# Strassen's seven products for eight in the query, key and value projections of a two-layer attention encoder

## The chip, the core and the metric

The kernel runs on one core of a Trainium2 chip. The metric is the time of one execution on the device, in microseconds. The core has five engines with queues of their own: TensorE (PE in the profile, with PEld for its weight loads), VectorE (DVE), ScalarE (ACT), GpSimd (POOL) and SyncE (SP), which here issues nearly all DMAs. Each engine takes its instructions in the order in which they stand in the built program.

## The reference

512 tokens of 1024 columns pass two layers, everything in float32. Layer A is a dilated sliding-window attention with three head groups, layer B a neighbourhood attention on an 8 x 64 grid. Each layer normalises its input, projects it to queries, keys, values and a gate, attends, multiplies by the SiLU of the gate, projects back and adds the input.

```python
hn = rms_norm(x, norm_gain[i])
proj = hn @ w_in              # layer A: 3 groups x (q, k, v) x 1024 columns, and 1024 of gate
q, k = rms_norm(q, q_gain[g]), rms_norm(k, k_gain[g])      # per head of 64
o, lse = dilated_group_attention(q, k, v, t5_bias, dilation, reach)
y = softmax-weighted sum of the three groups' o, times silu(gate)
x = x + y @ w_out
```

## The kernel before

**Head pairs.** The 16 heads are worked two at a time, as eight pairs (`hc` 0 to 7) of 128 columns. For one pair of layer A the projection has 1280 columns: 1024 of queries, keys and the values of groups 1 and 2, in two blocks of 512, then 128 of the values of group 0 and 128 of the gate. `main_a(hc)` (from L493) issues `project_qk` twice, then `v0_a` and `gate_a`.

**Precision.** A float32 product is made of three products of a rounded high half and a low half (`mm3`, L212, matmul line L206): high by high, high by low, low by high. The activations' halves `hn_h` and `hn_l` lie in SBUF from the start. The weights are read from memory as `wraw` (128 x 1024, three buffers), and `split` (L124) makes 128 x 512 halves of them: ACT rounds into `wh` (L127), then DVE or POOL subtracts into `wl` (L131), two of five on POOL. Both have four buffers, and `splits` keeps four ahead of TensorE.

**The projection.** In `project`, for each of eight k blocks of 128 rows one half `wh`, `wl` is multiplied with four tiles of 128 tokens into four accumulators in PSUM. ACT evacuates them scaled by the tokens' norm `rs_n` (L444), POOL squares (L268), DVE reduces (L269). `head_norm` makes the per-head scale in some 14 small steps (`rsqrt`, on POOL for keys, on DVE for queries) and DVE applies it (L290).

**The attention of a pair.** `k_a` turns the scaled keys on TensorE (`transpose4`) into `k12`. `q_a` turns the queries on DVE (L519) and through memory: four writes to `qd` (L532) and four reads (L538), after which `split_q` makes `k0h`, `q0h` on ACT (L559, L578) and `k0l`, `q0l` on DVE (L561, L580). `attn_a` issues two blocks of scores (`u` 0 and 1), DVE adds the bias and takes the minimum (L748, L759), ACT takes the exponential (L770), DVE the reciprocal (L608), ACT scales (L609). DVE turns the probabilities in 32 x 32 blocks (L681), and a `turner` sends them through memory (`td`, L690; `pt`, L694). `weigh` multiplies them by the values into `o`, and `put_y` multiplies by the gate (L629) and splits the result into `y_h` and `y_l` in SBUF, which `out_product` reads.

**The order.** `main` yields the large matmuls and `side` the rest. `run` weaves the two by a clock of TensorE's own work (`clock`, in nanoseconds): `yield "wait", key, n` lets a side step go n ns of that work after a stamp, and `later_on` does so for DMAs. So TensorE's order is fixed by hand, without regard to what the other engines really take; on the other engines the order comes from a scheduler that goes by estimates. In before, the weighing of a pair is held in `pending` and comes in the middle of the next pair's attention, the keys are turned 18,500 ns after their projection, and the values `v0` have two buffers.

```python
yield "wait", ("rawk", hc), 12500 if hc == 0 else 25500 if hc == 1 else 18500 if hc < NHC - 1 else 10000
...
pending.append(lambda: put_y(hc, weigh(), True, False))
```

Of the kernel before, what the change touches and what calls it, by code (L numbers as in the profile page):

```python
# [31 lines left out]
EXT = S + 64  # L32

# [9 lines left out]
def tile_hybrid_encoder(  # L43
# [45 lines left out]
    ones = cp.tile([P, S], F32R, name="ones")  # L89
    nc.vector.memset(ones.bitcast(F32), 1.0)  # L90

# [6 lines left out]
    v0 = [cp.tile([P, 4, P], F32, name=f"v0_{i}") for i in range(2)]  # L98
# [3 lines left out]
    x_all = big.tile([P, KT, S], F32, tag="y", name="x_all")  # L102
    y_l = big.tile([P, KT, S], F32R, name="y_l")
# [18 lines left out]
    turn, pool = [0], [2, 5]  # L122

    def split(raw, n):  # L124
        h = wp.tile([P, 512], F32R, tag="wh", name="wh", bufs=4)[:, :n]
        l = wp.tile([P, 512], F32R, tag="wl", name="wl", bufs=4)[:, :n]
        nc.scalar.copy(h, raw)  # L127
        turn[0] += 1
        to_pool = turn[0] * pool[0] % pool[1] < pool[0]
        eng = nc.gpsimd if to_pool else nc.vector  # L130
        eng.tensor_sub(l, raw, h.bitcast(F32))  # L131
        return h, l

    def blocks():

        for hc in range(NHC):
            b = hc * A_HC
            first = hc == NHC - 1
            yield from ((b + 512 * KT * (i ^ first), 512, KT) for i in range(2))
            if hc == NHC - 1:  # L140
                yield b - A_HC + 1152 * KT, 128, KT
            yield b + 1024 * KT, 128, KT
            if hc != NHC - 2:
                yield b + 1152 * KT, 128, KT
        yield from outs(A_OUT)
        for hc in range(NHC):
            b = B_IN + hc * B_HC
            yield from ((b, 384, KT), (b + 384 * KT, 128, KT))
        yield from outs(B_OUT)

    def outs(b):

        for n, ks in ((512, KT - 1), (384, KT - 1), (512, 1), (384, 1), (128, KT)):
            yield b, n, ks
            b += n * ks

    def loads():
        for off, n, ks in blocks():
            per = 1024 // n
            for k in range(0, ks, per):  # L160
                m = min(per, ks - k)
                yield w[:, off + k * n : off + (k + m) * n], m * n, n
# [3 lines left out]
    def raws():  # L166
        queue = []
        for src, cols, n in loads():
            raw = wp.tile([P, 1024], F32, tag="wraw", name="wraw", bufs=3)
            dst = raw[:, :cols]  # L170
            if not begun:
                nc.sync.dma_start(dst[:, :n], src[:, :n])
                begun.append(load_x(1, 2))
                dst, src = dst[:, n:], src[:, n:]
            nc.sync.dma_start(dst, src)
            if behind:
                behind.pop()()
            queue.append((raw, cols, n))
            if len(queue) > 2:
                yield queue.pop(0)  # L180
        yield from queue

    def splits():
        queue = []
        for raw, cols, n in raws():
            step = 384 if n == 384 else 512
            for c in range(0, cols, step):
                queue.append((*split(raw[:, c : c + step], step), min(n, step)))
                if len(queue) > 3:
                    yield queue.pop(0)  # L190
        yield from queue
# [7 lines left out]
    stamp = {(key, -1): 0 for key in ("k12", "q", "v", "qk")}  # L199
    stamp |= {(key, -i, "y"): 0 for key in ("ya", "yb") for i in (1, 2, 3)}  # L200
# [11 lines left out]
    def mm3(o, lh, ll, rh, rl, first, last):  # L212
        matmul(o, lh, rh, start=first, stop=False)
        matmul(o, lh, rl, start=False, stop=False)
        matmul(o, ll, rh, start=False, stop=last)
# [1024 lines left out]
```

## Time and profile before

| | before |
|---|---|
| runs | 868.75, 870.04 and 1035.45 us; median 870.04 |
| the profiled execution | span 866.1 us from the first to the last instruction |
| TensorE | busy 845.2 us (98%), 5515 matmuls |
| DVE, ACT, POOL | busy 520.8, 433.1 and 304.9 us |
| DMA | 145.43 MB, 168 GB/s on average |
| layer A's projections and attention | 0 to 532.3 us |
| layer A's output product | 532.3 to 592.2 us |
| layer B with its output product | 592.2 to 866.1 us |

The span is the profile's own time; a run's time has some 3 to 4 us around it. A busy share is an average over stages, and matmuls overlap their neighbours, so the distance from one start to the next tells a matmul's cost better than its duration. In the rows of groups stand the source line, the engine, the operation, what is written and read, the shapes, the count, then busy time and mean, then the idle time before and what ended it. In the rows of waits stand the total, how often, and the longest.

### The profile page before, as it was taken

Reading aid. Unit: us, or ns where it says so; the run is one execution under the profiler, and the core shown is the slowest. Engines: PE = TensorE matmul, PEld = TensorE weight load, DVE = VectorE, ACT = ScalarE, POOL = GpSimd, SP = SyncE. Lnnn points to the kernel's source line nnn. Section 1 sums busy time; section 2 is a strip of 40 time slices with the busy share of each in tenths; the row PEclk is TensorE's granted clock in tenths of the full one; section 3 lists DMA queues with packets and bytes.
Section 4 is the critical chain, followed back from the end, with each engine's and each line's share of the span. In section 5 each row is a group of like instructions: output and inputs, shape, how many; then the busy total and the mean of one; then the engine's idle time right before and its main releaser. Section 6 shows DMA issues by size and latency. Waiting matters only on the chain.

```text
span 866.1 us, 15411 instructions
## 1 busy us (share of the span) xinstructions
PE 845.2 (98%) x5515; PEld 702.3 (81%) x5515; DVE 520.8 (60%) x1339; ACT 433.1 (50%) x924; POOL 304.9 (35%) x493
## 2 busy tenths in 40 slices
PE   9999998999999999999998988999999999999998
PEld 7788886788787788788787876789988999889786
DVE  7355583765674665665664855538576656766643
ACT  7434552653553553553553464436366545665541
POOL 2342432441541541541542332111444345533511
PEclk9999999899999999999999999999999999999999
DMA  6355468379478479478469196255235654556223
GB/s 246 111 158 175 147 190 232 133 204 231 139 209 241 139 193 239 137 203 231 138 173 262 49 256 183 64 180 194 80 119 155 172 169 147 153 165 182 98 91 128
DMA packets 81212, 145.43 MB, mean 168 GB/s; under 512 B 7408, under 2 KB 41136, under 8 KB 81136
## 3 DMA queue, kind: packets, MB, share of 16 engines
q1 hardware_dynamic: 80848, 144.44, 56.7%
q8 instruction: 43, 0.70, 0.4%
q14 instruction: 33, 0.27, 0.1%
q10 hardware_dynamic: 288, 0.01, 0.0%
HBM read 111.20 MB, written 33.22 MB: 167 GB/s over the span
## 4 chain that ended last, share of the span: by engine, by line
PE 76%; DMA 9%; DVE 5%; ACT 4%; POOL 3%; issue 1%; SPq 1%; ACTq 0%; DVEq 0%; POOLq 0%
PE acc L206 64%; PE log L206 4%; PE o L206 4%; DMA wraw<-in_w 3%; DMA q<-qd 3%; PE tp L210 3%; DMA qd<-rawq 1%; DMA e<-l_d 1%; POOL wl L131 1%; POOL sq L268 1%; DVE rawq L519 1%; DVE rawq L290 1%; DMA pt<-td 1%; ACT wh L127 1%; ACT rawq L444 1%
## 5 line engine op out<-in xcount | busy, mean ns | idle before, releaser
L206 PE MATMUL acc<-wh,hn_h 128*128 128x512 f32 (+1 forms) x768 | 293.3, 382 | 4.4 <-ACT rawq L444 2.4
L127 ACT CAST wh<-wraw 128x512 fp32r<-128x512 f32 (+1 forms) x276 | 161.1, 589 | 251.4 <-PE acc L206 190.8
L206 PE MATMUL acc<-wl,hn_h 128*128 128x512 f32 (+1 forms) x768 | 285.4, 372 | 0.6 <-DVE wl L131 0.6
L206 PE MATMUL acc<-wh,hn_l 128*128 128x512 f32 (+1 forms) x768 | 285.6, 372 | 0.0
L131 POOL TENSOR_TENSOR wl<-wraw,wh 128x512 fp32r<-128x512 f32 (+1 forms) x110 | 141.1, 1283 | 389.5 <-ACT wh L127 367.2
L131 DVE TENSOR_TENSOR wl<-wraw,wh 128x512 fp32r<-128x512 f32 (+1 forms) x166 | 116.8, 704 | 116.2 <-ACT wh L127 111.9
L206 PEld LDWEIGHTS acc<-wh,hn_h 128*128 128x128 f32 x768 | 144.4, 188 | 33.4 <-issue 4.0
L206 PEld LDWEIGHTS acc<-wh,hn_l 128*128 128x128 f32 x768 | 144.3, 188 | 20.6
L206 PEld LDWEIGHTS acc<-wl,hn_h 128*128 128x128 f32 x768 | 144.5, 188 | 20.0 <-DVE wl L131 0.9
L206 PE MATMUL acc<-hn_h,wh 128*128 128x512 f32 x192 | 78.6, 409 | 2.6 <-ACT rawk L444 2.3
L206 PE MATMUL acc<-hn_l,wh 128*128 128x512 f32 x192 | 75.8, 395 | 0.0
L206 PE MATMUL acc<-hn_h,wl 128*128 128x512 f32 x192 | 75.8, 395 | 0.0
L770 ACT ACTIVATE p<-p,mn 128x512 f32<-128x512 f32 (+1 forms) x64 | 45.1, 705 | 59.9 <-DVE mn L759 59.9
L609 ACT ACTIVATE p<-p,mn 128x512 f32<-128x512 f32 (+3 forms) x128 | 69.4, 593 | 2.9 <-DVE mn L608 2.9
L269 DVE TENSOR_REDUCE ss<-sq 128x4 f32<-128x256 f32 (+1 forms) x96 | 48.4, 505 | 29.2 <-POOL sq L268 28.7
L268 POOL TENSOR_TENSOR sq<-rawk 128x256 f32<-128x256 f32 x64 | 42.7, 675 | 64.9 <-ACT rawk L444 51.9
L681 DVE STREAM_TRANSPOSE tr<-p 128x512 f32<-128x512 f32 (+1 forms) x80 | 53.7, 683 | 10.4 <-ACT p L609 6.2
L206 PE MATMUL acc<-y_h,wh 128*128 128x512 f32 x128 | 52.2, 408 | 0.0
L206 PE MATMUL acc<-y_h,wl 128*128 128x512 f32 x128 | 50.0, 391 | 0.0
L206 PE MATMUL acc<-y_l,wh 128*128 128x512 f32 x128 | 50.0, 390 | 0.0
L206 PEld LDWEIGHTS acc<-hn_h,wh 128*128 128x128 f32 x192 | 36.9, 192 | 13.0 <-ACT rawk L444 4.9
L206 PEld LDWEIGHTS acc<-hn_h,wl 128*128 128x128 f32 x192 | 36.6, 191 | 8.0
(130 smaller groups left out, 1075.8 us busy)
## 6 DMA issues: line engine op xcount, KB each, us to landing
wraw<-in_w SPq DMA_DIRECT2D x95, 512.0 KB
wraw<-in_w SPq DMA_DIRECT2D x38, 384.0 KB
td<-tr SPq DMA_DIRECT2D x56, 256.0 KB
pt<-td SPq DMA_DIRECT2D x56, 256.0 KB
qd<-rawq SPq DMA_DIRECT2D x32, 256.0 KB
q<-qd SPq DMA_DIRECT2D x32, 256.0 KB
td<-tr SPq DMA_DIRECT2D x24, 224.0 KB
pt<-td SPq DMA_DIRECT2D x24, 224.0 KB
```

The lines of the kernel that those rows point to most:

```text
L127: nc.scalar.copy(h, raw)
L131: eng.tensor_sub(l, raw, h.bitcast(F32))
L206: nc.tensor.matmul(o, l, r, **kw)
L210: nc.tensor.transpose(o, i, ident)
L268: nc.gpsimd.tensor_mul(sq.rearrange("p (c r) -> p c r", r=32) if ns == 8 else sq, v, v)
L269: nc.vector.tensor_reduce(ss[:, i * ns : (i + 1) * ns], sq.rearrange("p (a b) -> p a b", b=64), axis=AX.X, op=ALU.add)
L290: m = nc.vector.tensor_mul(v, v, by)
L444: nc.scalar.activation(dst, src, AF.Copy, scale=rs_n[:, i : i + 1])
L519: nc.vector.transpose(raw[:, :, i, :], raw[:, :, i, :])
L609: nc.scalar.activation(pr, pr, AF.Copy, scale=mn[:, 3:4])
L681: nc.vector.transpose(dst, src[:, :n].rearrange("p (i b k) -> p i b k", b=4, k=32))
L770: nc.scalar.activation(row, row, AF.Exp, bias=mn[:, 1:2], scale=-1.0, accum_out=mn[:, 2:3])
```

## The change

Pair 0 is projected as before. For pairs 1 to 7 the product of 512 tokens by 1024 rows by 1024 columns is cut into halves each way and made of seven half products (`product`): x11 by b11, x12 by b21, and five with sums of activation quarters (`mix_h`, `mix_l`, made once by `mix`) or sums of weight quarters (made for every pair by `Plan.mixed`, in place in `wraw`, six on POOL and two on DVE). In a product a half `wh`, `wl` meets two tiles of tokens and four k blocks. The seven results are put together on evacuation: two are copied by ACT (`keep`, `put11`), and DVE subtracts or adds the other five (`put_v`, `put_u`, `put12`, `put22`, `put21`), two tiles each. A pair's order on TensorE is: product 1, gate of the pair before, product 2 (same accumulators), products 3 to 6, value of the pair before, product 7.

The sums need activations that are scaled by their norm already: `scale_x`, `renorm` and `mix` do this during pair 0. Nine `wraw` buffers replace three, and two of three low halves go to POOL while `mixed` runs. To make room, biases, `v0`, `k12`, gates and others share buffers, and the attention output of pairs 0 to 5 is written to DRAM (`y_d`) unsplit and read back (`y_back`, `y_split`) in the last pairs. The weighing of a pair now follows its own attention, ahead of the next pair's keys. Squares go from POOL to ACT in layer A. The built program has 168 matmuls fewer, and 360 splits instead of 276; DVE, ACT and POOL have more instructions.

```diff
+H = S // 2
+KH = KT // 2
+SLOTS = 9
-    ones = cp.tile([P, S], F32R, name="ones")
+    y_d = dr.tile([P, NHC, S], F32, name="y_d")
+    mix_h = big.tile([P, 4, 4, H], F32R, tag="yh", name="mix_h")
+    mix_l = big.tile([P, 4, 4, H], F32R, tag="yl", name="mix_l")
...
+        def sum(self, at, dst, src, eng):
+            self.sums.setdefault(at, []).append((dst, src, eng))
...
+        def mixed(self, hc):
+            b, j = hc * A_HC, len(self.jobs)
+            b11, b21, b12, b22 = ([self.raw(b + 2048 * n + 1024 * i) for i in range(2)] for n in range(4))
+            gate = self.raw(b - A_HC + 1152 * KT)
+            v = self.raw(b - A_HC + 1024 * KT)
+            for part in (b11, gate, b21, b11, b11, b22, b12, v, b21):
+                for raw in part if isinstance(part, list) else [part]:
+                    self.use(raw, 128 if raw in (gate, v) else 512)
+            for i in range(2):
+                self.sum(j + 6 + 2 * i, b11[i], b12[i], nc.gpsimd)
+                self.sum(j + 12 + 2 * i, b11[i], b22[i], nc.vector)
+                self.sum(j + 16 + 2 * i, b21[i], b11[i], nc.gpsimd)
+                self.sum(j + 17 + 2 * i, b12[i], b22[i], nc.gpsimd)
...
+        for at, (raw, c, step, n) in enumerate(plan.jobs):
+            pool[0] = [2, 3] if start_jobs <= at < mixed_jobs else [2, 5]
+            for r in due.get(at, ()):
+                load(r)
+            for dst, src, eng in plan.sums.get(at, ()):
+                eng.tensor_add(dst.tile, dst.tile, src.tile)
+            queue.append((*split(raw.tile[:, c : c + step], step), n))
...
+    def product(acc, stat, open_, evac, guard=None):
+        if open_:
+            acc += [ps_acc.tile([P, 512], F32, tag="acc", name="acc") for _ in range(2)]
+        for k in range(KH):
+            ...
+            h, l = next(wsteps)
+            for i in range(2):
+                sh, sl = (t[:, P * i : P * i + P] for t in stat(k))
+                mm3(acc[i], sh, sl, h, l, open_ and k == 0, k == KH - 1, skip_group_check=True)
+                if k == KH - 1:
+                    evac(i, acc[i])
+                yield
...
-        nc.gpsimd.tensor_mul(sq.rearrange("p (c r) -> p c r", r=32) if ns == 8 else sq, v, v)
+        if on_act:
+            nc.scalar.activation(sq.rearrange("p (c r) -> p c r", r=32) if ns == 8 else sq, v, AF.Square)
+        else:
+            nc.gpsimd.tensor_mul(sq, v, v)
...
+    def scale_x():
+        pa = spread()
+        for k in range(KT):
+            xk = x_all[:, k, :]
+            nc.vector.scalar_tensor_tensor(xk, xk, ng[:, 0, k : k + 1], pa, op0=ALU.mult, op1=ALU.mult)
+    def renorm(k):
+        nc.scalar.copy(hn_h[:, k, :], x_all[:, k, :])
+        (nc.gpsimd if k % 2 else nc.vector).tensor_sub(hn_l[:, k, :], x_all[:, k, :], hn_h[:, k, :].bitcast(F32))
...
+        yield from product(a, hn(0, 0), True, keep, ("w", hc - 2))
+        yield from gate_a(hc - 1)
+        yield from product(a, hn(KH, 0), False, put11)
+        yield "q", hc - 1
+        box.append(raw_q())
+        yield from product(c, mixed(0), True, put_v)
+        yield from product(b, mixed(1), True, put_u)
+        yield from product(c, mixed(3), False, put12)
+        yield from product(b, mixed(2), False, put22)
+        normed(box[2], box[1], 8, "rawq", hc)
+        yield from v0_a(hc - 1)
+        yield from product(b, hn(KH, H), False, put21)
...
-        yield "wait", ("rawk", hc), 12500 if hc == 0 else 25500 if hc == 1 else 18500 if hc < NHC - 1 else 10000
+        yield "wait", ("rawk", hc), 10000
...
-        yield "wait", ("rawq", hc), 15000 if hc != 1 else 18000
+        yield "wait", ("rawq", hc), 12000
...
+        if permuted and hc < NHC - 2:
+            nc.vector.tensor_mul(gt, gt, o)
+            nc.sync.dma_start(y_d[:, hc, :], gt)
+            stamp["w", hc] = 0
+            return
...
+            if hc + 1 < NHC:
+                st["e", hc + 1] = bias_a(hc + 1)
+            yield from v_a(hc)
+            yield from q_a(hc + 1)
+            yield "wait", ("pt", hc, 1), 3000
+            if hc < NHC - 2:
+                put_y(hc, weigh(), True, False)
+                yield
+                return
...
         for hc in range(NHC):
-            if hc < NHC - 1:
-                yield from k_a(hc)
-                yield from chain(q_a(hc), v_a(hc))
-            ...
+            yield from k_a(hc)
+            yield from chain(st.pop(("land", hc)), attn_a(hc))
```

More of the change, by code (lines that the diff above doesn't have):

```diff
@@ L183, in splits @@
[L183 to L190, printed above, removed]
+                self.use(self.raw(off + k * n, m * n), n)
+        def sum(self, at, dst, src, eng):
+            self.sums.setdefault(at, []).append((dst, src, eng))
+            dst.used(at)
+            src.used(at)
@@ L452, in project_qk @@
             st["first"] = raw, ss
+            stamp["first",] = clock[0]
             return
@@ L544, in land @@
         def land():
-            yield "wait", ("rawq", hc), 27000 if hc != 1 else 30000
+            yield "wait", ("rawq", hc), 24000
             assert not left[0]
@@ L695, in read @@
                 self.left -= 1
+                if key and not self.left:
+                    stamp[key] = clock[0]
             for b in range(4):
```

418 lines of the change are left out of this document (243 added, 175 removed).

## The prediction

> **What bounds the kernel now.** I read the page first (busy shares and the chain that ended last), then what TensorE waited for, then one head pair of layer A, then the instructions of that pair.
>
> ```profile
> span 866.1 us, 15411 instructions
> PE 845.2 (98%) x5515; PEld 702.3 (81%) x5515; DVE 520.8 (60%) x1339; ACT 433.1 (50%) x924; POOL 304.9 (35%) x493
> DMA packets 81212, 145.43 MB, mean 168 GB/s; under 512 B 7408, under 2 KB 41136, under 8 KB 81136
> PE 76%; DMA 9%; DVE 5%; ACT 4%; POOL 3%; issue 1%; SPq 1%; ACTq 0%; DVEq 0%; POOLq 0%
> ```
> ```profile
> PE log L206 <- ACT q0h L578: 4.2, 1, 4.2
> PE tp L210 <- DVE rawk L290: 3.1, 1, 3.1
> ...
> PE acc L206 <- DVE wl L131: 0.6, 1, 0.6
> ```
> ```profile
> 196.60:260.80 64.20, 64.20 (x454) 52.18 (x454) 41.00 (x101) 31.58 (x61) 25.41 (x39) 1.00 0.70 192
> ```
>
> The kernel is bound by TensorE. It waits for the low weight halves 0.6 us in all, and the head pair from 196.6 to 260.8 us keeps it busy all 64.2 us, while VectorE (DVE) needs 41.0, ScalarE (ACT) 31.6 and GpSimd (POOL) 25.4 us. So fewer matmuls pay in full for as long as the others stay hidden. The two largest waits already name the links that matter below: the split of the query (q0h) and the key's scaling (rawk).
>
> **What the change removes.**
>
> ```profile
> 7.53 0.39 PE L206 MATMUL acc<-wh,hn_h 128*128 128x512 f32 x1
> ...
> 32.48 0.39 PE L206 MATMUL acc<-wh,hn_l 128*128 128x512 f32 x1
> ```
>
> These are the first and last of 111 matmuls in a row: (32.48 - 7.53) / 110 = 0.2268 us each. A pair's projection was 2 blocks x 8 k x 4 tiles x 3 = 192 of them, and is now 7 products x 4 k x 2 tiles x 3 = 168. That is 24 x 0.2268 = 5.44 us a pair, 38.1 us over seven pairs. TensorE's own work in a pair falls from 64.2 to 58.8 us. Nothing else leaves it.
>
> **What it adds to the other engines.** A pair now splits 32 half tiles of weights (28 for the products, 4 for gate and value) where it split 20, two in three on POOL instead of two in five. It adds eight sums of 128x1024 weights (six on POOL, two on DVE), and ten evacuations go to DVE. Squares move from POOL to ACT.
>
> ```profile
> L131 POOL TENSOR_TENSOR wl<-wraw,wh 128x512 fp32r<-128x512 f32 x81 | 110.6, 1365 | 317.4 <-ACT wh L127 301.2 <-DMA qd<-rawq 7.0 <-PE acc L206 4.8
> L268 POOL TENSOR_TENSOR sq<-rawq 128x512 f32<-128x512 f32 x32 | 33.2, 1058 | 21.6 <-ACT rawq L444 20.0 <-DMA wraw<-in_w 1.6
> L118 POOL TENSOR_TENSOR na<-na,nv 128x16 f32<-128x16 f32 x48 | 12.4, 259 | 3.4
> L131 DVE TENSOR_TENSOR wl<-wraw,wh 128x512 fp32r<-128x512 f32 x115 | 87.4, 760 | 86.4 <-ACT wh L127 82.8 <-PE acc L206 3.6
> L290 DVE TENSOR_TENSOR rawk<-rawk,rs 128x256 f32<-128x256 f32 x64 | 28.8, 511 | 16.9 <-POOL rs L120 16.2
> L759 DVE CUSTOM_DVE_ANT_1 p<-log,e,mn 128x256 f32<-128x256 f32 x64 | 28.6, 478 | 0.0
> L748 DVE CUSTOM_DVE_ANT_0 p<-log,e 128x256 f32<-128x256 f32 x32 | 12.2, 420 | 3.1 <-PE log L206 3.1
> L681 DVE STREAM_TRANSPOSE tr<-p 128x512 f32<-128x512 f32 x68 | 46.9, 703 | 10.2 <-ACT p L609 6.0 <-DMA td<-tr 3.2 <-DMA e<-l_d 0.5
> L488 DVE TENSOR_TENSOR vt<-acc,rs_trj 128x512 f32<-128x512 f32 x8 | 5.5, 683 | 1.2 <-PE acc L206 1.2
> L127 ACT CAST wh<-wraw 128x512 fp32r<-128x512 f32 x196 | 119.9, 619 | 177.8 <-PE acc L206 120.5 <-DMA wraw<-in_w 33.6 <-issue 9.0
> ```
>
> No sum of 1024 columns is in the trace. From below it costs one 512-column subtraction (1.37 on POOL), from above twice that (2.7); as twice the 512-column multiply it is 2.1. I take 2.6 on POOL, near the upper end since a subtraction of two tensors is the nearest row, and 1.5 on DVE (twice 0.76). POOL then goes from 25.4 to 25.4 + 13.3 x 1.37 + 6 x 2.6 - 7 (squares) = 52 us of 58.8, and DVE from 41.0 to about 41 + 10 x 0.68 + 2 x 1.5 = 51 us. ACT gains 12 x 0.62 = 7.4 us and squares, and sheds evacuations: about 40. Each still fits, but two run at 85% or more, in a fixed order.
>
> The transfers stay small beside this. The weights are loaded once as before (ten loads a pair, now into nine buffers instead of three), and the attention output adds six writes and two reads, 3 MB in all beside 145 MB. I cost them nothing, as TensorE waited for no weight load; what they do to SP's order is counted below. Two multiplies by the row scale leave DVE and the pairs' splits of y move to the last pair, ahead of the output product: nothing either, while that pair's own waits cover them, and three subtractions of 1.4 us on POOL if not.
>
> What matters more is the cover. Both kernels keep four halves of wh and wl. A half used to feed 4 tiles x 3 = 12 matmuls (2.7 us); in a product it feeds 2 x 3 = 6 (1.36 us). The lead of four halves shrinks from 10.9 to 5.4 us. I therefore walked the changed program's order on each engine through one pair.
>
> **Wait 1, at the key's transposes.** Let T = 0 be when the second half of the pair's last product has been used, which frees the buffer that POOL's next subtraction needs.
>
> ```profile
> 217.19 0.36 PE L206 MATMUL log<-k0h,q0h 64*128 64x192 f32 x2
> ...
> 219.19 0.50 PE L206 MATMUL acc<-wh,hn_h 128*128 128x512 f32 x1
> ...
> 222.14 1.97 PE L206 MATMUL o<-pt,rawk 128*64 128x128 f32 x32
> 223.93 1.90 PE L206 MATMUL o<-pt,v 128*64 128x256 f32 x16
> 225.76 0.50 PE L206 MATMUL acc<-wh,hn_h 128*128 128x512 f32 x1
> ```
>
> A block of scores takes 219.19 - 217.19 = 2.0 us and the weighing (o) 225.76 - 222.14 = 3.6 us. TensorE's order from T = 0 is 45 matmuls (10.2), the value's transposes (0.35), the weighing (3.6): it stands at the key's transposes at T = 14.2. They need the scaled key, and that has two chains.
>
> On POOL, the key's 14 small norm steps stand behind five subtractions and four weight sums: 0.6 (cast) + 5 x 1.37 + 4 x 2.6 + 14 x 0.26 = 21.5, then four scalings on DVE (4 x 0.51): T = 23.5. Before, the key's transposes came over 18 us after its projection; now 10.
>
> The second chain is the query's, since the split of k0 and q0 stands ahead of that scaling on DVE.
>
> ```profile
> 203.58 3.35 SPq L532 DMA_DIRECT2D qd<-rawq  x4
> ```
> ```profile
> 205.54 4.60 DMA qd<-rawq
> ...
> 210.22 3.22 DMA q<-qd
> ```
> ```profile
> 213.46 1.14 ACT L559 CAST k0h<-q 128x512 fp32r<-128x512 f32 x1 [4.38 <-DMA q<-qd]
> ```
> ```profile
> 214.63 1.14 DVE L561 TENSOR_TENSOR k0l<-q,k0h 128x512 fp32r<-128x512 f32 x1 [7.50 <-ACT k0h L559]
> 215.68 0.75 DVE L580 SCALAR_TENSOR_TENSOR q0l<-q,gk,q0h 128x512 fp32r<-128x512 f32 x1
> ```
>
> SP's queue holds the new write of the attention output after the first of the four query writes. It waits for the weighing (done at T = 8.7) and a 0.7 us multiply, so the other three writes, and all that is queued behind them (a weight load, the query's reads), go out from about T = 9.8. Three issues take 2.5, landing 4.6, the read 3.2, then k0h, k0l and q0l 3.0, and the scalings 2.0: T = 25.1. So TensorE waits 9.3 to 10.9 us. If a sum cost no more than one subtraction (4.9 less) and the DMAs landed in half the time, it would be 4. I take 7.0, midway, since queues behind a late TensorE have some of it done already.
>
> **Wait 2, at the first reused accumulator.** From the key's transposes TensorE runs 87 matmuls (19.7), 0.7 of transposes and two blocks of scores (4.0) up to the fourth product: 24.4 us. The low half of that product's first weights stands on DVE behind both blocks of the softmax: eight tiles x (0.42 + 0.48 + 0.17 reads) = 8.6, five transposes 3.5, eight reciprocals 1.3, four subtractions 3.0, two sums 3.0, two evacuations 1.4 and 1.7 of reduces and gate. That is 22.5 us, begun when the first scores are there at 6.4, less some cover: 27 to 30. I take a wait of 2.5, between none (were ACT's exponentials and DVE perfectly packed) and 5.5.
>
> **The clock after a wait.**
>
> ```profile
> 149.20:156.00 6.80, 4.47 (x78) 3.53 (x79) 4.58 (x14) 3.44 (x8) 3.04 (x3) 0.52 0.51 178
> ```
>
> The 4.2 us wait for q0h, just before this window, is followed by 6.8 us at a granted clock of 0.52. So a long wait is paid twice: between nothing and 3.3 us more. (6.8 x 0.48). I take the middle, 1.7, once a pair.
>
> **The sum.** Six pairs with both waits: 6 x (7.0 + 2.5 + 1.7) = 67.2. The first mixed pair and the start, where x is scaled, split again and mixed on DVE ahead of the key's weights: 4 (between 0 and 8). The old q0h wait and its slow clock go, as they sit where the new ones are counted: 4.2 + 3.3 = 7.5. Layer B and the output products keep their work: 0, between -3 and 3. 866.1 - 38.1 - 7.5 + 67.2 + 4 = 891.7 us of span. The median of the runs, 870.0, lies 3.9 above this profile's span: 895.6, 2.9% slower.
>
> **The rivals.** (a) All waits stay hidden: 866.1 - 38.1 - 7.5 + 3.9 = 824. For it: no engine is over 90% full. Against it: POOL's norm steps end at T = 21.5, 7 us after TensorE stands at the transposes, even with every transfer landed. [...] (c) The waits at their upper bounds, 10.9 + 5.5 + 3.3 in each of six pairs: 866.1 - 38.1 - 7.5 + 118.2 + 8 + 3.9 = 951, as DVE, late at one place, meets the next late.
>
> **How the numbers follow.** My case has 0.72: its waits may add up to between 6 and 17 us a pair, so 864 to 930. (a) has 0.06, (b) 0.12, (c) 0.10. A measurement of this kernel tells about 2% from no change: 853 to 887. Faster takes (a), most of (b) and the lower tail of my case: 0.17. Slower takes (c) and two thirds of my case: 0.58; 0.25 is left between. The range for 8 times in 10 is 845 to 940.
>
> **What would show it.** TensorE's waits should list the key's transposes behind DVE's scaling of rawk, some 7 us each in six pairs, and low weight halves (wl) behind DVE and POOL, together some 60 us where they were 4. The granted clock should fall to a half after each key wait. A pair should take 68 to 72 us. SP should stand at the attention output's write with query writes behind it. I am wrong if a pair takes under 62 us, if POOL's norm steps end before TensorE reaches the transposes, or if the time is lost at the start or in the last pair instead.

## The result, and the profile after

The changed kernel takes 1037.64 us (median of four runs, 1033.76 to 1039.01) against 869.62 us (median of four) for the kernel before, run beside it on the same chip. That is 1.193 times as long, 95% interval 1.190 to 1.197; this comparison leaves out one disturbed run of the kernel before, of 1035.45 us. The prediction had the direction right, 895.6 us, but its range ended at 940. The profiled run of the changed kernel, 1033.76 us, has a span of 1032.0 us, so 1.8 us lie around a span here, not 3 to 4.

The page of the profiled execution, first lines and chain:

```profile
span 1032.0 us, 15480 instructions
PE 866.4 (84%) x5347; PEld 700.9 (68%) x5347; DVE 639.5 (62%) x1411; ACT 492.3 (48%) x1026; POOL 490.5 (48%) x576
PE 38%; DMA 12%; DVE 6%; ACT 5%; issue 2%; SPq 1%; POOL 1%; DVEq 0%; ACTq 0%; POOLq 0%
```

TensorE has the 168 matmuls less that were promised (5347 for 5515), worth 38.1 us. Yet it is busy for longer, 866.4 us for 845.2: what is left of its work took 866.4 - (845.2 - 38.1) = 59.3 us longer. And it is idle for 1032.0 - 866.4 = 165.6 us where it was idle for 20.9. So the whole of the change in the span is -38.1 + 59.3 + 144.7 = 165.9 us. No engine is full: VectorE, the busiest beside TensorE, stands at 62%.

Where TensorE waited, in the changed kernel (total, times, longest):

```profile
PE tp L273 <- DVE rawk L376: 68.0, 8, 14.2
PE o L269 <- DMA pt<-td: 22.5, 4, 7.7
PE acc L269 <- POOL wl L137: 21.4, 16, 3.4
PE acc L269 <- DVE wl L137: 21.2, 12, 5.9
PE o L269 <- DMA qd<-rawq: 7.3, 2, 4.4
PE o L269 <- ACT v L742: 5.0, 1, 5.0
PE o L269 <- issue: 4.9, 1, 4.9
PE acc L269 <- ACT wh L133: 4.7, 6, 3.0
```

Three places hold nearly all of it: the key's transposes (68.0 us), the weighing `o` (39.7 us over four rows) and the weight halves (47.3 us over three). The rows name the reads of the probabilities (`pt`) for 22.5 us of the weighing, and the values (`v`) for 5.0. Before, the largest single wait in the trace was 4.2 us.

The windows of two head pairs, of layer A's output product and of layer B up to its own (columns: window, length, busy time of PE, PEld, DVE, ACT and POOL, granted clock, DMA share, GB/s):

```profile
321.70:405.60 83.90, 67.26 (x430) 52.44 (x430) 54.04 (x110) 38.52 (x74) 49.12 (x49) 0.88 0.57 157
405.60:489.50 83.90, 65.78 (x429) 51.13 (x428) 51.71 (x112) 38.56 (x74) 46.80 (x46) 0.90 0.54 146
702.10:758.50 56.40, 56.40 (x429) 45.83 (x429) 29.49 (x80) 27.65 (x56) 9.20 (x12) 1.00 0.49 159
758.50:974.80 216.30, 215.83 (x1359) 195.41 (x1358) 135.25 (x408) 125.33 (x323) 83.40 (x176) 1.00 0.48 142
```

A head pair takes 83.9 us where it took 64.2. Its engines are as full as the prediction had them (DVE 51.7 to 54.0 us for 51 predicted, POOL 46.8 to 49.1 for 52, ACT 38.5 for 40), and the clock stands at 0.88 to 0.90. Layer B is untouched: its 216.3 us stand beside this row of the kernel before:

```profile
592.00:809.60 217.60, 216.34 (x1360) 195.63 (x1359) 140.31 (x408) 125.70 (x323) 91.55 (x180) 1.00 0.49 143
```

All the loss is in layer A's pairs, as the prediction said, but it is more than six times as large: 165.9 us of span where 25.6 were forecast.

**The key's transposes, read closely.** In the pair from 405.6 us on, TensorE is through with its products at 431.1 and stands 8.38 us. The timeline there, engine by engine (start, duration, engine and line, what it writes from what, and in brackets the idle time before it and what ended it):

```profile
414.42 0.30 SPq L702 DMA_DIRECT2D qd<-rawq  x1
426.22 0.34 SPq L798 DMA_DIRECT2D y_d<-gt  x1
426.61 2.13 SPq L702 DMA_DIRECT2D qd<-rawq  x3
```
```profile
428.41 2.40 POOL L250 TENSOR_TENSOR wraw<-wraw 128x1024 f32<-128x1024 f32 x1
...
435.99 0.22 POOL L126 TENSOR_TENSOR rs<-rs,na 128x16 f32<-128x16 f32 x1
```
```profile
436.32 1.06 ACT L729 CAST k0h<-q 128x512 fp32r<-128x512 f32 x1 [6.08 <-DMA q<-qd]
```
```profile
437.42 1.05 DVE L731 TENSOR_TENSOR k0l<-q,k0h 128x512 fp32r<-128x512 f32 x1 [6.05 <-ACT k0h L729]
438.38 0.74 DVE L750 SCALAR_TENSOR_TENSOR q0l<-q,gk,q0h 128x512 fp32r<-128x512 f32 x1
439.04 1.42 DVE L376 TENSOR_TENSOR rawk<-rawk,rs 128x256 f32<-128x256 f32 x4
```
```profile
439.52 1.48 PE L273 MATMUL tp<-ident,rawk 128*128 128x128 f32 x4 [8.38 <-DVE rawk L376]
```

Both chains of the prediction are there. SP issues the first query write at 414.42 and the other three only at 426.61, behind the write of the attention output: 12.2 us later. The query's read therefore lands at 436.3, its split takes VectorE to 439.1, and the key's scaling stands behind that split. GpSimd's norm steps end at 436.2, behind the weight sums. The two chains end within a few microseconds of each other. In five of the eight pairs the scaling starts as the query's split ends, 2.5 to 4.2 us after the norm steps; in two it starts as the norm steps end, and in the last pair with neither. What mending either chain is worth cannot be read from this alone.

### The profile page after: what moved, and what is told of

Its sections match the earlier page's. It is cut to its first block, busy times and chain, and to the rows that moved or that the text cites. A ratio compares the mean times of both kernels' runs of the same rounds, so it can differ in the third digit from the quotient of the medians.

```text
span 1032.0 us, 15480 instructions
## 1 busy us (share of the span) xinstructions
PE 866.4 (84%) x5347; PEld 700.9 (68%) x5347; DVE 639.5 (62%) x1411; ACT 492.3 (48%) x1026; POOL 490.5 (48%) x576
## 2 busy tenths in 40 slices
DMA packets 82367, 148.59 MB, mean 144 GB/s; under 512 B 7536, under 2 KB 41264, under 8 KB 82160
## 4 chain that ended last, share of the span: by engine, by line
PE 38%; DMA 12%; DVE 6%; ACT 5%; issue 2%; SPq 1%; POOL 1%; DVEq 0%; ACTq 0%; POOLq 0%
PE acc L269 30%; DMA wraw<-in_w 4%; PE o L269 3%; DMA pt<-td 3%; PE tp L273 2%; PE log L269 2%; DMA td<-tr 2%; ACT wh L133 1%; DMA qd<-rawq 1%; DVE wl L137 1%; DMA q<-qd 1%; DMA e<-l_d 1%; ACT p L779 1%; ACT p L959 1%; DVE wraw L250 1%
## 5 line engine op out<-in xcount | busy, mean ns | idle before, releaser
L137 POOL TENSOR_TENSOR wl<-wraw,wh 128x512 fp32r<-128x512 f32 (+1 forms) x205 | 270.9, 1327 | 417.6 <-ACT wh L133 395.6
L269 PE MATMUL acc<-wl,hn_h 128*128 128x384 f32 (+1 forms) x488 | 180.9, 371 | 15.5 <-DVE wl L137 14.3
L269 PE MATMUL acc<-wh,hn_h 128*128 128x384 f32 (+1 forms) x488 | 185.8, 381 | 0.7 <-ACT wh L133 0.5
L269 PE MATMUL acc<-wh,hn_l 128*128 128x384 f32 (+1 forms) x488 | 179.6, 368 | 0.0
L250 POOL TENSOR_TENSOR wraw<-wraw 128x1024 f32<-128x1024 f32 x42 | 102.2, 2434 | 40.2 <-DMA wraw<-in_w 17.2
L269 PE MATMUL acc<-wl,mix_h 128*128 128x512 f32 x224 | 93.7, 418 | 27.2 <-POOL wl L137 20.2
L269 PEld LDWEIGHTS acc<-wl,hn_h 128*128 128x128 f32 x488 | 93.9, 192 | 28.2 <-DVE wl L137 17.4
L269 PEld LDWEIGHTS acc<-wh,hn_h 128*128 128x128 f32 x488 | 93.9, 192 | 17.5 <-issue 4.1
L269 PE MATMUL acc<-wh,mix_h 128*128 128x512 f32 x224 | 90.9, 406 | 4.2 <-ACT wh L133 4.2
L269 PE MATMUL acc<-wh,mix_l 128*128 128x512 f32 x224 | 90.4, 404 | 0.0
L269 PEld LDWEIGHTS acc<-wl,mix_h 128*128 128x128 f32 x224 | 43.6, 195 | 45.8 <-POOL wl L137 27.0
L269 PE MATMUL o<-pt,rawk 128*64 128x128 f32 (+2 forms) x400 | 36.7, 352 | 34.6 <-DMA pt<-td 22.5
```

The costliest lines, as they stand in the source:

```text
L250: eng.tensor_add(dst.tile, dst.tile, src.tile)
L269: nc.tensor.matmul(o, l, r, **kw)
```

## The experiments

Sixteen kernels were run. "The waits" are those of TensorE; "slow work" is TensorE's busy time above 845.2 - 38.1 = 807.1 us, which is what the reduced work would take at the kernel before's pace. A half tile is one pair of `wh` and `wl`, which a product uses up in six matmuls, 1.36 us. The theories: (1) two queue chains of nearly equal length make the key late; (2) the weight halves come too late, because their lead in time was halved or because GpSimd and VectorE carry the sums; (3) each longer wait is paid again by a half clock. A fourth came up on the way: (4) the transfers of the probabilities are late for the weighing.

**1 to 3: the key's two chains.** The output's write goes out later on SP:

```diff
-            nc.sync.dma_start(y_d[:, hc, :], gt)
+            later_on(6000, partial(nc.sync.dma_start, y_d[:, hc, :], gt))
```

> The write of the attention output is issued later on SP, behind all four query writes; nothing else moves. In the changed kernel the scaled key waits for two chains at once: in pairs 2 to 7 the query split starts when its read has landed, and POOL's norm steps end only 2 to 4 us before the scaling starts. Theory 1 (two queue chains of nearly equal length, SP's and POOL's): the SP chain goes, POOL's takes over; the waits at the key's transposes fall from 68 to about 50 us, the time from 1038 to 1010 to 1025. Rival (SP's queue alone decides, POOL is only late because TensorE is): those waits fall to about 20 us and the half clock after them goes too, time about 970. Rival (transfers or the weight halves decide): no change, 1030 to 1040.

Measured: 1028.43 us, key waits 59.9 us. This is the way of theory 1, but less than it expected in both, and the gain in time (9 us) is hardly clear of noise. SP's chain is mended and GpSimd's, a few microseconds shorter, takes its place: the scaling now starts as the norm steps end in six of the eight pairs.

The key's rsqrt goes to VectorE, away from the sums:

```diff
-        rsqrt(nc.vector if ns == 8 else nc.gpsimd, rs[...], ...)
+        rsqrt(nc.vector, rs[...], ...)
```

> The key's rsqrt (14 small steps a pair) runs on VectorE instead of GpSimd, so it no longer stands behind the weight sums; SP's order stays as it is. Theory 1 (two chains of nearly equal length): only the first pair's wait of 14 us falls, since there the query had landed long before; in pairs 2 to 7 SP's chain stays, so about 1015 to 1030, with key waits of about 50 us. Rival (POOL's chain alone decides): key waits under 20 us and about 970.

Measured: 996.57 us, between the two theories; the key's waits, 12.7 us, are as low as the rival had them. The waits at the two places the chains lead to:

```profile
PE log L269 <- ACT q0h L748: 14.3, 6, 3.8
PE tp L273 <- DVE rawk L376: 12.7, 2, 11.3
```

The key's wait is left in the first pair alone (11.3 us). In the others the scaling now stands ahead of the query's split in VectorE's order, so the late query holds up only the scores that need it, six times 2.4 us. The SP chain reached the key's transposes only through VectorE's order of instructions, as the prediction had it; my expectation for this run forgot that the edit changes that order.

> Both edits together: the output's write behind the query writes, and the key's rsqrt on VectorE. Theory 1: only now do the waits at the key's transposes go, from 68 to under 20 us, and with them the half clock behind them (about 3 us for each of seven), so 955 to 975. Rival (the work given to VectorE and GpSimd is too much in any order): the waits come back at the weight halves and at the weighing, and the time stays above 1000.

Measured: 974.19 us, key waits 12.2 us. The two chains together are worth 63 us (58.5 in the spans: 40.3 of idle time, and 18.2 of slow work, which falls from 59.3 to 41.1). The key's waits alone fell by 56 us, but 9 came up at the weighing, which now waits 48.5 us, and 4 at the scores; the halves still cost 45.8.

**4: the sums.**

```diff
-                eng.tensor_add(dst.tile, dst.tile, src.tile)
+                pass
```

> The weight sums are left out (the products use plain weight blocks, so a part of the computation is missing); POOL loses 42 x 2.43 = 102 us and VectorE 14 sums. Theory 2 (GpSimd and VectorE are overfilled): the waits for the weight halves fall from 47 to under 20 us and the norm steps end 10 us earlier, but SP's chain at the key stays: about 980 to 1000. Rival (the shorter lead of four half-used weight halves makes those waits, not the sums): the waits for the halves stay near 40 us, and the time only falls to 1015 to 1025, by what the first pair's key wait and pieces of the others are worth.

Measured: 957.15 us, more than either side expected. The waits for the halves fall from 47.3 to 24.4 us, so the sums make about half of them; the key waits fall from 68 to 17, as GpSimd's norm steps come earlier and the scaling stands ahead of the query's split in six pairs, as in run 2. The larger surprise is what is left: with none of the sums' work the kernel is still 10% slower than before.

**8: the lead alone.** The kernel before, with two buffers for the halves of the weights instead of four:

```diff
-        h = wp.tile([P, 512], F32R, tag="wh", name="wh", bufs=4)[:, :n]
-        l = wp.tile([P, 512], F32R, tag="wl", name="wl", bufs=4)[:, :n]
+        h = wp.tile([P, 512], F32R, tag="wh", name="wh", bufs=2)[:, :n]
+        l = wp.tile([P, 512], F32R, tag="wl", name="wl", bufs=2)[:, :n]
...
-                if len(queue) > 3:
+                if len(queue) > 1:
```

> The kernel before with two buffers for the high and low weight halves instead of four, and two in the queue: the lead falls from 10.9 to 5.4 us, as in the changed kernel, with none of its added work. Theory (the lead is the main cause of the waits for the halves): they rise from 0.6 to some 40 us, time 900 to 930. Rival (the added sums and subtractions are): under 10 us, 870 to 882.

Measured: 920.90 us, 53.8 more than the kernel before beside it. Its waits (`wh`, `wl` are the halves; lines are those of the kernel before):

```profile
PE acc L206 <- ACT wh L127: 22.3, 15, 6.0
PE acc L206 <- DVE wl L131: 22.0, 30, 1.5
PE acc L206 <- POOL wl L131: 5.2, 8, 0.9
```

That is 49.5 us where there were 0.6, and the time that the first theory expected, with no sum, no Strassen product and no added subtraction. So the lead is a cause by itself: in time, a queue of four halves of which each feeds six matmuls instead of twelve is a queue of two. In the spans the 53.3 us are 34.3 of idle time, as other waits of the kernel before are gone, and 19.1 of longer busy time, though the mean granted clock is 0.991 for 0.992. So slow work is not all the clock's. Run 8 prices the lead in the kernel before; what it is worth among the other waits of the changed kernel no run separates.

**5, 15, 6: the weighing and the clock.** With the key mended the weighing waits longest. What it waits for, as far as the rows tell, is mostly the transposed probabilities (`pt`), which go through DRAM. SP's queue in the changed kernel ahead of the weighing at 420.2 us:

```profile
402.37 0.84 SPq L239 DMA_DIRECT2D wraw<-in_w  x2
403.44 2.10 SPq L881 DMA_DIRECT2D pt<-td  x3
406.91 0.35 SPq L239 DMA_DIRECT2D wraw<-in_w  x1
408.96 0.30 SPq L881 DMA_DIRECT2D pt<-td  x1
```

The last read is issued behind a weight load, at 408.96, and its packets (of 2048 bytes) end at 419.3, ten microseconds later and just ahead of the weighing. The windows of 25 us that end where the weighing starts, kernel before first, then the changed one (last columns: clock, DMA share, GB/s):

```profile
391.90:416.90 25.00, 25.00 (x181) 20.17 (x179) 14.63 (x28) 9.44 (x18) 6.29 (x5) 1.00 0.75 207
```
```profile
395.20:420.20 25.00, 19.15 (x85) 15.05 (x84) 19.10 (x34) 11.07 (x20) 14.26 (x11) 1.00 0.99 260
```

The 16 DMA engines are full there, at 0.99 for 0.75. The nine weight loads that open a pair are due within 14 half tiles (some 19 us), because a load is issued 12 half tiles ahead of its use and several blocks are needed at once for the sums. Over the whole pairs on either side the share is only 0.54 to 0.57, by their rows above.

```diff
-        return 4 if raw.first < start_jobs else 12 if raw.first < mixed_jobs else 6
+        return 4 if raw.first < start_jobs else 7 if raw.first < mixed_jobs else 6
```

> On top of the run with both queue edits (974 us): weight loads of the mixed pairs are issued 7 half tiles ahead of their use instead of 12, so that the bunch of nine loads a pair comes some 7 us later, behind the transposes of the probabilities instead of among them. There the 16 DMA engines are full for 27 us ahead of the weighing, and its last 2048-byte packets run until the moment it starts. Theory (full DMA engines delay the weighing, in all 48 us): waits at the weighing fall to under 25 us, the half clock behind them partly too, so 935 to 955. Rival (the order of SP's queue or the value's transposes delay it): they stay, 970 to 980; or the loads come too late for the products and casts wait for weights: above 980.

Measured: 940.20 us on top of the two queue edits: the weighing's waits fall from 48.5 to 15.3 us, and the time by 34. The waits for the halves rise from 45.8 to 61.0 us, 13.2 of it in one wait at the start of the first mixed pair. The edit changes both what fills the DMA engines and what stands ahead of the reads in SP's queue. The same window in one pair of it, where the weighing no longer waits:

```profile
338.60:363.60 25.00, 23.28 (x104) 18.67 (x104) 21.28 (x35) 12.57 (x24) 14.59 (x12) 1.00 0.91 247
```

> On top of write behind the queries and rsqrt on VectorE, with four halves and nine load buffers: loads 5 half tiles ahead (12: 974 us, 7: 940 us). Theory (full DMA engines): the weighing's waits go from 17 to under 8 us, 928 to 938. Rival (loads too late): the waits for the halves rise from 61 to 75 us or more, 945 to 960.

Measured: 945.87 us; waits at the weighing 13.1 us, at the halves 60.4 as with 7 ahead. Neither theory fits: the gain is used up at 7, and the 6 us more are within the noise (run 10 below).

For the clock, matmuls that nothing needs fill the wait:

```diff
             o, v0 = bank("o"), st.pop("v0")
+            for _ in range(26 if hc < NHC - 2 else 0):
+                nc.tensor.matmul(o, hn_h[:, 0, :P], hn_h[:, 1, :], start=True, stop=True)
```

> On top of the run with both queue edits (974 us): 26 matmuls of 128x512 that nothing needs stand ahead of the weighing in pairs 1 to 6 (26 x 0.227 = 5.9 us at full clock), where TensorE waits 3 to 8 us; the result is the same. Theory 3 (a wait of some microseconds is paid a second time by a half clock behind it): the records of half clock after the weighing go, some 3 us each in six pairs, while the fillers mostly fit into the wait, so 955 to 965. Rival (the half clock comes whatever TensorE does, or its slow matmuls are hidden under the next wait anyway): 974 to 985, as the fillers add what does not fit.

Measured: 965.56 us, at the edge of what theory 3 expected. The page's line:

```profile
PE 874.5 (91%) x5503; PEld 709.4 (74%) x5503; DVE 700.2 (73%) x1587; ACT 490.1 (51%) x1026; POOL 444.2 (46%) x352
```

156 matmuls more are worth 35.4 us, and took the place of 36.1 us of waits at the weighing (48.5 to 12.4). The rest of TensorE's work shrank from 848.2 to 874.5 - 35.4 = 839.1 us: 9.1 us, or 1.5 us for each weighing. The mean granted clock rises from 0.947 to 0.969. So the half clock behind a wait is real and was bought back here by matmuls that nothing needs, at half of the price I had set in this expectation.

**7, 9 to 12, 14, 16: more lead, and what it costs elsewhere.** Five buffers and five in the queue for the halves, paid for with eight load buffers for nine:

```diff
-SLOTS = 9
+SLOTS = 8
...
-... tag="wh", name="wh", bufs=4)        # wl and ones alike
+... tag="wh", name="wh", bufs=5)
...
-            if len(queue) > 3:
+            if len(queue) > 4:
```

> On top of the run with both queue edits (974 us): five buffers for the high and the low weight halves instead of four, and five in the queue, paid for with eight instead of nine load buffers. The lead of the halves over TensorE grows from 4 x 1.36 = 5.4 to 6.8 us. Theory (the short lead makes the waits for the halves, 43 us over 30 waits): each of the larger ones falls by up to 1.4 us, those waits by 20 to 30 us in all, time 940 to 955. Rival (VectorE and GpSimd are late by many microseconds at these places, whatever the lead): under 10 us, 965 to 975.

Measured: 977.53 us. The waits for the halves fell, from 45.8 to 37.2 us, and the weighing's rose, from 48.5 to 63.7. A miss: I had counted one side only.

> The three edits that helped (write behind the queries, rsqrt on VectorE, loads 7 half tiles ahead: 940 us) together with five weight halves and eight load buffers. With the DMA engines no longer full ahead of the weighing, the longer lead should now be visible in the time. Theory (lead): waits for the halves fall from 61 to about 35 us, 912 to 925. Rival (what is won at the halves is lost at the weighing again, as with five halves alone): 935 to 945.

Measured: 953.99 us, 14 slower than with four halves. Halves 35.3 us for 61.0, weighing 53.2 for 15.3. SP's own waits between 80 and 590 us point to the reason; with four halves and nine load buffers, then with five and eight:

```profile
SPq L239 <- DVE wl L137: 44.6, 8, 23.1
SPq L239 <- POOL wl L137: 26.1, 15, 4.7
```
```profile
SPq L239 <- DVE wl L137: 100.7, 6, 21.2
SPq L239 <- POOL wl L137: 39.2, 14, 9.3
```

SP stands 140 us instead of 71 at a weight load whose buffer is not yet free, and the transfers of the probabilities stand behind it.

> On top of write behind the queries, rsqrt on VectorE and five weight halves with eight load buffers (954 us at 7 ahead): loads are issued 4 half tiles ahead, so the bunch comes 4 us later still. Theory (bunched weight loads fill the DMA engines ahead of the weighing): the waits there fall from 49 to under 20 us and the time to 915 to 930, if the loads still arrive in time. Rival (they are too late now: casts wait for loads): waits for the high halves above 20 us, 950 or more.

Measured: 940.00 us; weighing 38.5 us, halves 34.2. The waits at the weighing fall by 14.7 us and the time by 14, about half of what was expected, with the two intervals still touching (1.069 to 1.096 and 1.092 to 1.102 of the kernel before). The loads do not come too late (waits for high halves 5.4 us).

> The three edits (940 us), and the two GpSimd sums of the second half's block, which stood between half tiles 16 and 18 of a pair, moved to half tiles 21 and 23; with the other two and four to five subtractions they asked for some 15 us of GpSimd in 6 half tiles, which TensorE uses up in 8.2 us. Theory (a bunch on GpSimd, not its sum over the pair, makes the wait of about 3 us at the first reused accumulator): that wait goes in six pairs, 18 us of waits, 918 to 930. Rival (VectorE's softmax ahead of it makes the wait, as predicted): no change, 935 to 943.

```diff
-                self.sum(j + 16 + 2 * i, b21[i], b11[i], nc.gpsimd)
+                self.sum(j + 21 + 2 * i, b21[i], b11[i], nc.gpsimd)
```

Measured: 946.25 us, no gain, and the wait of about 3 us stays (2.84 and 3.36 us in two pairs). But the edit moved nothing: in the traces of this run and of run 5 every engine has the same instructions in the same order, by line and tile; the order on the engines beside TensorE is the scheduler's. GpSimd's bunch of sums is still there, so the run decides nothing about it. It does show the noise: the same order took 940.20 and 946.25 us.

> All of it: write behind the queries, rsqrt on VectorE, loads 7 ahead, five halves with eight load buffers, and the two sums moved. If each cause is its own, the waits left are some 30 us and the half clock 15: 895 to 912. It would not come under the kernel before (868), since 38 us saved stand against more than 60 of waits and slow clock left. Rival (the work given to VectorE and GpSimd finds a new place to be late): 920 to 940.

Measured: 953.77 us over four runs, ratio to the kernel before 1.096 (1.092 to 1.100): as in run 9. Here too every engine's order is that of run 9, so the moved sums are not tested. The time expected, 895 to 912 us, is missed, and the rival's as well.

> Write behind the queries, rsqrt on VectorE, loads 7 ahead, five halves, and the weight sums left out (a part of the computation is missing). It bounds what the sums cost once the queues are in order. Theory (with the chains and the lead mended the sums are what is left): 870 to 885. Rival (the split of 32 half tiles and the lead, not the sums): 895 to 910.

> Write behind the queries, rsqrt on VectorE, five halves, loads 4 ahead, and the weight sums left out (a part of the computation is missing); 922 us at 7 ahead, with 52 us of waits at the weighing. Theory (with the weighing mended little is left but the saved matmuls): 860 to 880. Rival (the weighing waits for the same transfers wherever the loads stand): 910 to 925.

Measured: 922.18 and 902.51 us. Even with none of the sums' work, the queues in order, five halves and later loads, the kernel stays 3.9% (3.2 to 4.6) slower than before. In the second run 31.3 us of waits at the weighing, 15.2 at the halves and 25.4 us of slow work are left. The first run lies above both expectations, the second between its two. I take it that the attention chain of the pair, through DRAM and back, doesn't fit under the shorter pair; no run shows this by itself.

**13: whose queue.** The weight loads of a pair are issued by ScalarE:

```diff
-        nc.sync.dma_start(dst, src)
+        eng = nc.scalar if start_jobs <= raw.first < mixed_jobs else nc.sync
+        eng.dma_start(dst, src)
```

> On top of write behind the queries, rsqrt on VectorE and loads 7 ahead (940 us): the ten weight loads of a pair are issued from ScalarE's queue instead of SP's, so the transposes of the probabilities no longer stand behind them, while the bytes and the time of the loads stay. Theory (order of SP's queue delays the weighing): its waits, 17 us, fall to under 8, and 925 to 935. Rival (the DMA engines are full, whoever issues): the waits stay at 12 to 25 us, 937 to 950, ScalarE having 70 issues more.

Measured: 984.02 us, and yet the waits at the weighing are nearly gone, 15.3 to 5.8 us. ScalarE seems to pay instead, with its casts behind its loads: TensorE waits 77.7 us for halves where it was 61.0, among them 21.1 for high halves where it was 5.1:

```profile
PE acc L270 <- ACT wh L133: 21.1, 14, 5.1
```

Ahead of a weighing the DMA engines are still 0.88 busy:

```profile
287.90:312.90 25.00, 20.54 (x80) 15.86 (x78) 16.35 (x28) 9.70 (x17) 11.20 (x8) 0.86 0.88 248
```

So the order in SP's queue may have a large share in theory 4. How much of the weighing's wait is the full engines and how much the order stays open: the slower products of this run also gave the transfers more time.

No version came under the kernel before. The best that compute the whole are 940 us (run 5, and run 14).

## Why the prediction was wrong

The direction, the place (layer A's pairs, layer B at nothing) and the mechanism of wait 1 were right. The largest failures were the weighing, put at nothing, and the slow clock, put at 10 us. Term by term, in TensorE's time:

| term | predicted | measured |
|---|---|---|
| matmuls saved | -38.1 | -38.1 (168 fewer, at the same 0.2268 us) |
| key's transposes | 42 (6 x 7.0) | 68.0 in 8 waits |
| weight halves | 15 (6 x 2.5) and 4 at the start | 47.3 in 34 waits, 9.2 of them at the start |
| weighing | 0 | 39.7 in 8 waits |
| slow clock (measured: all slow work) | 10 (6 x 1.7) | 59.3, some 44 of it the clock's |
| other waits, less those of the kernel before | -7.5 | 10.6 - 20.9 = -10.3 |
| sum | 25.6 | 165.9 |

**Key's transposes.** Right within its own bounds. Six of the eight waits are 6.7 to 9.5 us, where the bounds were 4 and 10.9 and I took 7.0. Run 1 showed that GpSimd's chain takes over when SP's goes. The other way round isn't shown, since run 2 also took the scaling out from behind the query's split; the two edits together took away 56 us of the 68. Mis-sized was the count: the first of the eight is 14.2 us and the last 5.2, and I had put 4 us on the start as a whole and nothing on the last pair.

**The sums.** Priced well from the rows that were there: 2.6 us on GpSimd and 1.5 on VectorE, measured 2.43 and 1.64:

```profile
L250 POOL TENSOR_TENSOR wraw<-wraw 128x1024 f32<-128x1024 f32 x42 | 102.2, 2434 | 40.2 <-DMA wraw<-in_w 17.2 <-DVE wraw L250 10.2 <-DVE mn L778 5.9
L250 DVE TENSOR_TENSOR wraw<-wraw 128x1024 f32<-128x1024 f32 x14 | 23.0, 1643 | 0.1
```

**Weight halves.** Waits of the forecast size came, 1.9 to 3.4 us a pair for 2.5, but in another place and by another link, so the size was partly luck. The prediction put them 87 matmuls behind the key's transposes, on a low half that VectorE makes behind its softmax. There TensorE waited 0.8 to 1.7 us in five pairs, 4.0 in one and hardly at all in one. The longer waits stand 50 to 77 matmuls behind the transposes, in four of the seven pairs in the first product with a mixed activation, as here:

```profile
370.81 1.72 DVE L250 TENSOR_TENSOR wraw<-wraw 128x1024 f32<-128x1024 f32 x1
...
373.42 2.10 DVE L137 TENSOR_TENSOR wl<-wraw,wh 128x512 fp32r<-128x512 f32 x1
```
```profile
372.61 2.37 POOL L250 TENSOR_TENSOR wraw<-wraw 128x1024 f32<-128x1024 f32 x1 [1.16 <-DVE mn L778]
374.94 3.12 POOL L137 TENSOR_TENSOR wl<-wraw,wh 128x512 fp32r<-128x512 f32 x2
```
```profile
376.70 0.80 PE L269 MATMUL acc<-wl,mix_h 128*128 128x512 f32 x1 [3.36 <-POOL wl L137]
```

The low half comes from GpSimd, right behind a weight sum that begins as VectorE's sum ends (370.81 + 1.72 = 372.53). VectorE's sum stands among the softmax's work, but the link over GpSimd's sum was not in the walk, and no run tests it.

The term as a whole was mis-sized, 19 us for 47.3. I had worked out that the lead shrinks from 10.9 to 5.4 us and then looked for one place where that hurts. Run 8 prices the lead by itself at 49.5 us of waits in the kernel before, and run 4 puts about half of the changed kernel's waits down to the sums. A cover that is halved should be priced along the whole stage, not where the walk happens to find a bunch.

**Weighing: the failed step.** "I cost them nothing, as TensorE waited for no weight load" was true of weight loads and wrong of what shares their queue and engines. The row of a pair that I had quoted showed a DMA share of 0.70, and the 25 us ahead of a weighing 0.70 to 0.78 in three pairs; bunching nine loads there fills the rest. The bytes hardly changed (148.59 MB for 145.43); their place in time did, and run 5 won 34 us by moving the loads alone. Whether the full engines or the order in SP's queue weigh more stays open.

**Slow clock: the second failed step.** I had one half-clock stretch a pair at half price. The changed kernel has about three a pair, behind the key, the weighing and the mixed products, as in these two windows, around the weighing at 336 us and around the wait for a half at 376 us:

```profile
334.50:341.30 6.80, 5.13 (x40) 4.55 (x42) 0.00 (x0) 0.00 (x0) 5.85 (x3) 0.52 0.15 48
375.40:382.20 6.80, 5.50 (x81) 4.35 (x81) 6.74 (x8) 1.14 (x2) 5.30 (x4) 0.52 0.68 233
```

So the clock's term is not a share of one wait but follows the number of long waits. By the records of the granted clock, the changed kernel has 24 stretches of half clock within its span and 59.3 us of slow work, run 3 has 18 and 41.1, run 5 has 12 and 33.7. Not all slow work is the clock's. TensorE is busy for 103.6 us within the 24 stretches, where the kernel before was for 11.3 us. A matmul starts every 0.43 us there (as at 377.72, 378.15 and 378.57 us) instead of every 0.227, so by estimate 49 us are lost to the clock for 5 before: some 44 of the 59.3.

Of the rivals, (c), all waits at their upper bounds, was the nearest with 951, and still 87 us short: it bounded two places and one stretch of half clock a pair, and there are three places and about three stretches. (a) fell. (b), VectorE and GpSimd slowing each other, was not run by itself. In the rows above VectorE's subtraction takes 2.10 us beside GpSimd's sum, where the mean in the kernel before was 0.76. In that kernel's pair from 196.6 us, two subtractions on VectorE that began while GpSimd ran one took 1.45 and 1.58 us, the other ten 0.65 to 0.70. How much of the waits for the halves comes from this stays open.

Of its own signs the two waits did head the list (110.6 us with the low halves, for some 60), and the clock fell to a half at each key wait, but a pair takes 83.9 us where 68 to 72 were expected. None of the signs that the prediction named as proving it wrong came true: a pair is longer than 62 us, the norm steps end after TensorE stands at the transposes, and the loss is spread over the pairs. They guarded its direction, not its size.

## What to carry to other kernels

When a change makes each buffer feed half as many matmuls, count the lead in microseconds and price its loss over the whole stage; in the kernel before that alone cost more than the matmuls saved here (53.8 us against 38.1). In a stage with a long serial loop of its own (query through DRAM, probabilities through DRAM), list for every transfer on a shared queue what is now issued ahead of it, and look at the DMA share of the 25 us before its use (0.99 here), not of the whole stage (0.54 to 0.57). And price every new wait of some 3 us or more with its slow clock, at each place: 22 of the 23 waits of 2.8 us or more had a stretch of half clock at them here. Before reading a run, see in its trace that the edit changed the order it was meant to change.

## What was not expected of the hardware

By the records of the granted clock, the half clock comes in stretches of 3.4, 6.8 and 10.2 us, and one of 13.7. Their starts lie whole multiples of 3.41 us apart, the 24 of the changed kernel and the three of the kernel before. In the changed kernel's pairs 22 of the 23 waits of 2.8 us or more have such a stretch beginning at them or within 2 us of their end, and the one left out is 3.26 us long; of the 18 between 0.6 and 1.4 us only one has, of 0.93 us, next to a longer wait. In run 5 all five waits of 3.35 us and more have one, and of the seven between 2.0 and 3.1 us two; but three shorter ones, of 1.45, 1.70 and 1.81 us at key transposes and scores, have one too. So these runs show no sharp limit between 1.4 and 3.3 us. With starts on such a grid it may depend on where the wait falls, which no run tests.

Run 8 shows the other side. It waits 49.5 us for halves, mostly some 1.5 us or less at a time, and its mean granted clock is 0.991, where the changed kernel has 0.919. Its short waits hardly touched the clock, but they were not paid by their own length alone: TensorE was busy 19.1 us longer. Part of that may be that the matmul behind a wait has nothing to overlap with: it takes 0.39 us where matmuls in a row start every 0.227, 9 us by estimate over 53 waits. The rest is not explained.
